# One weight sum of each Strassen set made in the SBUF ring by an accumulating load instead of DRAM steps, the other sum steps at lower rates

## The chip, the core and the metric

The kernel runs on one core of one Trainium2 chip. The metric is the device time of one execution in microseconds (us); lower is better. A core has a matrix engine (TensorE, "PE" in the profile), a vector engine (DVE), an activation engine (ScalarE, "ACT"), GpSimd ("POOL") and SyncE ("SP"). POOL and SP are used here mostly to issue DMAs. Each engine takes its instructions in program order: one that waits holds up all that stand behind it on that engine.

## The reference

One layer of a decoder in float32, 512 positions of width 1024. What matters for this case is that it is a row of large matrix products with weights that lie in DRAM:

```python
proj = x @ w_in[i]                       # q, k, v of three attention branches, and the gates
...                                      # differential, stick-breaking and dilated attention
merged = (g[:, :, 0] * (o_da @ w_branch_da) + g[:, :, 1] * (o_sb @ w_branch_sb)
          + g[:, :, 2] * (o_dl @ w_branch_dil))
x = layer_norm(DEEPNORM_ALPHA * x + merged @ w_out[i], ln1_g[i], ln1_b[i])
hid = jax.nn.relu(x @ w_up[i])           # 1024 -> 4096
c = jnp.square(hid) @ w_down[i]          # 4096 -> 1024
ple = jax.nn.sigmoid(x @ w_ple_gate[i]) * (p[i] @ w_ple[i])
x = layer_norm(DEEPNORM_ALPHA * x + c + ple, ln2_g[i], ln2_b[i])
```

The branch attentions are the kernel's part up to about 690 us, the MLP (`w_up`, `w_down`) the part from there to the end.

## The kernel before

**Products.** Nearly every large product is done as a 2x2 block product with seven multiplications instead of eight (Strassen's scheme in Winograd's form). Products 1, 2 and 4 use a plain block of the weights; products 5, 6, 7 and 3 use sums of two to four weight blocks. One up set (`up_parts(m)`, m = 0 to 7) and one down set (`down_parts`, m = 0 to 6 as seven products) each take four plain blocks and four sums. In an up set the four sums are called operands 0, 1, 2 and 3, and the plain blocks that stand alone "11", "12" and "22". The text writes u0, u1, ... for up sets and d0, d1, ... for down sets. `group_items` does the same for the queries of the three dilated groups (the tile-group sets, `wq`).

**Chunks and the two rings.** A weight block of 128x1024 float32 (512 KB) is a *chunk*. SP loads it into one of six `raw` slots (`fill`, L194 to L216; the DMA is L213). Then ACT casts it to the high part, `wh<-raw` (L262), and DVE takes the low part, `wl<-raw,wh` (L264); this is called splitting the chunk. `wh` and `wl` have five slots each. PE multiplies each block three times (high by high, high by low, low by high). A `raw` slot is loaded anew only when the chunk in it has no more uses; a `wh`/`wl` slot is written again only when PE has read it.

**Sums in DRAM.** The sums are made beforehand in DRAM tiles (`qsum`, `usum`, `dsum` and a few more) by DMAs that POOL issues: `issue` writes a plain copy (L1249) or an accumulating DMA, which adds a block to what is there (L1247). `sum_steps` lists them: an up set has the eight steps

```python
                yield a1, w[2], False
                yield a3, w[0], False
                yield a1, w[3], True
                yield a3, w[2], True
                yield a2, a1, False
                yield a2, w[0], True
                yield a4, a2, False
                yield a4, w[1], True
```

where True means accumulate. A step that uses what an earlier one wrote waits for that DMA to land. Two sets (in the later part of the list) are worked on in turn, a step of each. The finished sum is loaded by SP like any weight block. How far the list runs is set by a credit: each item of the main loop adds its size times a rate, or 0.78 once the gate products are done, and a step is issued for each whole credit. Besides, every step waits for the fourth last `wl` subtraction that the program wrote ahead of it, so that POOL doesn't run ahead of the main stream.

**Sums in the ring.** A second way exists for the value pairs and the gates: `then_add(c, src)` (L171 to L178). After chunk `c` has been split, POOL issues an accumulating DMA of another weight block into the very `raw` slot that `c` lies in (L176), and a later chunk is split from this slot. The slot stays taken until then. In the gates, such a slot is split for the second time four chunks after the first time or later.

**Order.** One Python loop over items writes all instructions. Each engine's order follows from it; nothing is reordered at run time.

Of the kernel before, what the change touches and what calls it, by code (L numbers as in the profile page):

```python
# [10 lines left out]
F32 = mybir.dt.float32  # L11
# [7 lines left out]
P = 128  # L19
# [36 lines left out]
def trunk(tc, a, out):  # L56
    nc = tc.nc
    es = ExitStack()
    with es:
# [108 lines left out]
        def chunk(src, w):  # L168
            return chunk_of(load(src, w))
# [114 lines left out]
        items = []  # L284
# [66 lines left out]
        HC = slice(256, 512)  # L351
        qsum = [[dram.tile([P, 1024], F32, name=f"qsum{m}_{i}") for i in range(4)] for m in range(3)]

        def group_items(gi, pairs):
# [380 lines left out]
        def seven(forms, operand, bank_of, done):  # L735

            cs = {}
            for p in (1, 2, 7, 6, 4, 5, 3):
                for r in range(2):
# [467 lines left out]
        ND = 8  # L1207
        gsum = [[dram.tile([P, 1024], F32, name=f"gsum{m}_{i}") for i in range(2)] for m in range(2)]
        usum = [[dram.tile([P, 1024], F32, name=f"usum{m}_{i}") for i in range(4)] for m in range(ND)]
        dsum = [[dram.tile([P, 1024], F32, name=f"dsum{m}_{i}") for i in range(4)] for m in range(ND - 1)]  # L1210

        def sum_steps():
            def up_steps(sums, w, flat=False):
                w = [w[i] if flat else w[i].rearrange("p k n -> p (k n)") for i in range(4)]
                a1, a2, a3, a4 = sums
# [17 lines left out]
            def down_steps(m):  # L1233
                w = [a["wd"][m, i].rearrange("p k n -> p (k n)") for i in range(4)]
                b1, b2, b3, b4 = dsum[m]
                yield b1, w[0], False
                yield b3, w[1], False
                yield b1, w[1], True
                yield b3, w[3], True
                yield b2, b1, False  # L1240
                yield b2, w[3], True
                yield b4, b2, False
                yield b4, w[2], True

            def issue(o, i, plus):
                if plus:
                    i = nc.gpsimd.dma_start(o, i, accum_op=OP.add, max_dma_last_dim=4096)  # L1247
                else:
# [7 lines left out]
                         for n in range(2) for m in range(2))  # L1256
            todo.extend(up_steps(qsum[m], a["wq"][m]) for m in range(3))
            for n in range(3):
                todo.extend(two_steps(msum[n][m], a["wgm"][n, m]) for m in range(2))
                if n:  # L1260
                    todo.append(up_steps(bsum[2 * (n == 1)], a["wbq"][int(n == 1)]))
# [50 lines left out]
        def up_parts(m):  # L1312
# [5 lines left out]
            def operand(n):  # L1318
                src = usum[m][n] if isinstance(n, int) else wu[{"11": 0, "12": 1, "21": 2, "22": 3}[n]].rearrange(
                    "p k n -> p (k n)")  # L1320
                cs[n] = chunk(src, 1024)

            def pair(j):
# [21 lines left out]
                def part_a():  # L1345
# [632 lines left out]
        def dil_head(hd):  # L1978
# [198 lines left out]
        for n, it in enumerate(items):  # L2177
# [199 lines left out]
```

## Time and profile before

| what | value |
|---|---|
| time, median of three runs | 1036.29 us (1035.86 to 1038.79) |
| time of the profiled execution | 1029.26 us |
| its span in the profile | 1027.5 us |
| granted TensorE clock | 0.999 |
| PE busy | 1014.6 us (99%) |
| DVE busy / ACT busy | 794.4 us (77%) / 614.7 us (60%) |
| POOL busy | 208.8 us (20%) |
| DMA moved | 275.99 MB, 269 GB/s on average |

The busy time of an engine is the time in which one of its instructions ran. The profiled execution lies 7.03 us below the median of the three runs; 1.76 us of it lie outside the span. Of the DMA traffic, 135.08 MB went through the queue that POOL issues to and 138.99 MB through that of SP.

### The profile page before, as it was taken

The page shows a single profiled execution, that of the slowest core. Times are in us where ns is not written, and L with a number is a line of the kernel's source. Part 1 is how long each engine was busy: PE and PEld are TensorE (multiplying, and loading weights), DVE is VectorE, ACT ScalarE, POOL GpSimd, SP SyncE. Part 2 cuts the span into 40 slices and gives each one's busy share as a digit, 9 for nine tenths or more (in the row PEclk, how much of TensorE's full clock was granted, in tenths as well). Part 3 has the DMA queues.
Part 4 walks back from the last instruction along what each step waited for, and adds up shares of the span by engine and source line. Part 5 has one row for each costly group of instructions (what it writes and reads, how often), then busy time and mean ns, then how long its engine had stood idle before and what let it go on. Part 6 is the DMA issues. An engine that isn't in the chain of part 4 may idle for free.

```text
span 1027.5 us, 15644 instructions
## 1 busy us (share of the span) xinstructions
PE 1014.6 (99%) x5626; PEld 879.0 (86%) x5626; DVE 794.4 (77%) x1411; ACT 614.7 (60%) x1055; POOL 208.8 (20%) x311
## 2 busy tenths in 40 slices
PE   9999999999999999999999999999999999999997
PEld 6888887888998898888888888889999999999786
DVE  6888697788657776886788885897778778768785
ACT  7566566775544656566655733866666656556551
POOL 0232320121412123111121130222121211111101
PEclk9999999999999999999999999999999999999999
DMA  8999993888999999879999893799999999998932
GB/s 312 286 306 288 259 271 96 209 206 259 288 319 283 253 287 276 220 201 263 352 291 273 294 323 109 182 248 355 338 323 332 318 324 350 327 332 263 297 148 82
DMA packets 79885, 275.99 MB, mean 269 GB/s; under 512 B 9816, under 2 KB 10600, under 8 KB 79808
## 3 DMA queue, kind: packets, MB, share of 16 engines
q0 software_dynamic: 37712, 135.08, 52.4%
q1 hardware_dynamic: 41520, 138.99, 36.6%
q8 instruction: 44, 0.72, 0.3%
q10 hardware_dynamic: 576, 0.92, 0.2%
q14 instruction: 33, 0.27, 0.1%
HBM read 267.59 MB, written 116.42 MB: 374 GB/s over the span
## 4 chain that ended last, share of the span: by engine, by line
PE 92%; DVE 4%; DMA 1%; ACT 1%; issue 1%; DVEq 0%; SPq 0%; ACTq 0%
PE mm L87 9%; PE mm L88 9%; PE mm L89 9%; PE at L1431 4%; PE at L1430 4%; PE at L1432 4%; PE at L752 2%; PE at L751 2%; PE at L750 2%; PE mm L750 2%; PE mm L751 2%; PE mm L752 2%; PE at L89 2%; PE at L88 2%; PE at L87 2%; PE at L1042 1%
## 5 line engine op out<-in xcount | busy, mean ns | idle before, releaser
L264 DVE TENSOR_TENSOR wl<-raw,wh 128x1024 fp32r<-128x1024 f32 (+1 forms) x274 | 330.2, 1214 | 111.4 <-ACT wh L262 110.2
L262 ACT CAST wh<-raw 128x1024 fp32r<-128x1024 f32 (+1 forms) x274 | 283.7, 1042 | 206.9 <-PE mm L88 104.3
L87 PE MATMUL mm<-xhT,wh 128*128 128x512 f32 (+1 forms) x254 | 95.5, 376 | 1.1 <-DVE dl_k L346 1.1
L89 PE MATMUL mm<-xhT,wl 128*128 128x512 f32 (+1 forms) x254 | 94.4, 371 | 0.0
L88 PE MATMUL mm<-xlT,wh 128*128 128x512 f32 (+1 forms) x254 | 94.1, 370 | 0.0
L1431 PE MATMUL at<-wl,hh 128*128 128x512 f32 x188 | 73.8, 393 | 1.0 <-DVE wl L264 1.0
L1430 PE MATMUL at<-wh,hh 128*128 128x512 f32 x188 | 73.9, 393 | 0.5 <-ACT hid L1402 0.5
L1432 PE MATMUL at<-wh,hl 128*128 128x512 f32 x188 | 73.2, 389 | 0.0
L87 PE MATMUL mm<-x1hT,wh 128*128 128x256 f32 x256 | 72.8, 284 | 0.0
L88 PE MATMUL mm<-x1lT,wh 128*128 128x256 f32 x256 | 72.4, 283 | 0.0
L89 PE MATMUL mm<-x1hT,wl 128*128 128x256 f32 x256 | 72.4, 283 | 0.0
L87 PEld LDWEIGHTS mm<-xhT,wh 128*128 128x128 f32 x254 | 47.9, 189 | 8.9 <-issue 1.2
L89 PEld LDWEIGHTS mm<-xhT,wl 128*128 128x128 f32 x254 | 47.8, 188 | 8.3
L88 PEld LDWEIGHTS mm<-xlT,wh 128*128 128x128 f32 x254 | 47.9, 189 | 7.5
L1247 POOL DMA_DIRECT2D usum<-in_wu_dram x32 | 27.0, 843 | 134.5 <-DVE wl L264 61.5
L87 PEld LDWEIGHTS mm<-x1hT,wh 128*128 128x128 f32 x256 | 48.9, 191 | 1.9
L88 PEld LDWEIGHTS mm<-x1lT,wh 128*128 128x128 f32 x256 | 48.9, 191 | 1.5
L89 PEld LDWEIGHTS mm<-x1hT,wl 128*128 128x128 f32 x256 | 48.9, 191 | 0.0
L1247 POOL DMA_DIRECT2D dsum<-in_wd_dram x28 | 24.1, 860 | 106.4 <-DVE wl L264 30.1
L1432 PEld LDWEIGHTS at<-wh,hl 128*128 128x128 f32 x188 | 35.3, 188 | 7.6
L1430 PEld LDWEIGHTS at<-wh,hh 128*128 128x128 f32 x188 | 35.5, 189 | 7.1 <-ACT hid L1402 0.7
L1431 PEld LDWEIGHTS at<-wl,hh 128*128 128x128 f32 x188 | 35.5, 189 | 7.0 <-DVE wl L264 1.3
(676 smaller groups left out, 2857.3 us busy)
## 6 DMA issues: line engine op xcount, KB each, us to landing
usum<-in_wu_dram POOLq DMA_DIRECT2D x48, 512.0 KB, 8.9
dsum<-in_wd_dram POOLq DMA_DIRECT2D x42, 512.0 KB, 8.9
raw<-usum SPq DMA_DIRECT2D x32, 512.0 KB, 8.5
raw<-dsum SPq DMA_DIRECT2D x28, 512.0 KB, 7.8
raw<-in_wt_dram SPq DMA_DIRECT2D x26, 512.0 KB, 7.8
raw<-in_wd_dram SPq DMA_DIRECT2D x25, 512.0 KB, 9.7
raw<-in_wu_dram SPq DMA_DIRECT2D x24, 512.0 KB, 8.3
qsum<-in_wq_dram POOLq DMA_DIRECT2D x18, 512.0 KB, 8.9
```

Of the source, the lines that this page charges most:

```text
L87: nc.tensor.matmul(ps, wh, xh, start=start, stop=False, skip_group_check=True)
L88: nc.tensor.matmul(ps, wh, xl, start=False, stop=False, skip_group_check=True)
L89: nc.tensor.matmul(ps, wl, xh, start=False, stop=stop, skip_group_check=True)
L262: i = nc.scalar.copy(h, raw)
L264: i = nc.vector.tensor_sub(lo, raw, h.bitcast(F32))
L750: nc.tensor.matmul(ps, h[:, q], c["h"][:, n], start=go, stop=False, skip_group_check=True)
L751: nc.tensor.matmul(ps, h[:, q], c["l"][:, n], start=False, stop=False, skip_group_check=True)
L752: nc.tensor.matmul(ps, lo[:, q], c["h"][:, n], start=False, stop=end, skip_group_check=True)
L1247: i = nc.gpsimd.dma_start(o, i, accum_op=OP.add, max_dma_last_dim=4096)
L1430: nc.tensor.matmul(ps, h[:, q], c["h"][:, s], start=go, stop=False, skip_group_check=True)
L1431: nc.tensor.matmul(ps, h[:, q], c["l"][:, s], start=False, stop=False, skip_group_check=True)
L1432: nc.tensor.matmul(ps, lo[:, q], c["h"][:, s], start=False, stop=end, skip_group_check=True)
```

## The change

In three families of sets one of the four sums is no longer made in DRAM:

- in the three `wq` sets, product 3's sum is made from product 6's chunk by `then_add` (plus `w[1]`);
- in all eight up sets, operand 2 is made from the plain chunk "11" (plus `wu[2]`), and for this "11" is loaded and split ahead of "12" (before: "12", "11", then 2, 1, 0, 3, "22");
- in the down sets d0 to d4, product 4's sum is made from product 6's chunk (plus `wd[m, 2]`). The order of products stays 1, 7, 6, 4, 5, 2, 3. d5 and d6 keep their four sums.

So 32 of 208 POOL steps in DRAM go (6 of 24 for `wq`, 16 of 64 for up, 10 of 56 for down), 16 loads by SP go, and 16 accumulating DMAs into `raw` slots come, issued by POOL. The number of matmuls stays the same. The rates at which the remaining steps are issued are lowered (1.0 to 0.8; 2.8, 2.3 and 3.3 to 2.6, 2.1 and 2.7; 0.78 to 0.6), and the dilated head 3 is put off by one more item.

```diff
@@ group_items
-                    at = {5: 0, 6: 1, 7: 2, 3: 3}.get(p)
-                    cs[p] = [chunk(w[{1: 0, 2: 1, 4: 3}[p]] if at is None else qsum[gi][at], 1024)]
+                    at = {5: 0, 6: 1, 7: 2}.get(p)
+                    cs[p] = [then_add(cs[6][0], w[1]) if p == 3 else
+                             chunk(w[{1: 0, 2: 1, 4: 3}[p]] if at is None else qsum[gi][at], 1024)]
...
-                    items[-1]["rate"] = 1.0
+                    items[-1]["rate"] = 0.8
...
-            it.setdefault("rate", 2.8 if j < 12 else 2.3 if j < 52 else 3.3)
+            it.setdefault("rate", 2.6 if j < 12 else 2.1 if j < 52 else 2.7)
@@ sum_steps
+                a3 = sums[2] if third else None
                 yield a1, w[2], False
-                yield a3, w[0], False
+                if third:
+                    yield a3, w[0], False
                 yield a1, w[3], True
-                yield a3, w[2], True
+                if third:
+                    yield a3, w[2], True
                 yield a2, a1, False
                 yield a2, w[0], True
-                yield a4, a2, False
-                yield a4, w[1], True
+                if fourth:
+                    yield sums[-1], a2, False
+                    yield sums[-1], w[1], True
...
-                yield b4, b2, False
-                yield b4, w[2], True
+                for b4 in dsum[m][3:]:
+                    yield b4, b2, False
+                    yield b4, w[2], True
...
-                todo.append(up_steps(usum[m], a["wu"][m]) if kind == "u" else down_steps(m))
+                todo.append(up_steps(usum[m], a["wu"][m], False, True) if kind == "u" else down_steps(m))
@@ up_parts
+                if n == 2:
+                    cs[n] = then_add(cs["11"], wu[2].rearrange("p k n -> p (k n)"))
+                    return
...
-                    operand(("12", "11")[j])
+                    if j == 0:
+                        operand("11")
+                        operand("12")
@@ down_parts
-                            cs[p] = [down_chunk(m, p) for m in ms]
+                            cs[p] = [down_chunk(m, p) if p != 4 else
+                                     then_add(cs[6][n], a["wd"][m, 2].rearrange("p k n -> p (k n)"))
+                                     for n, m in enumerate(ms)]
@@ the dilated heads, and the main loop
-            for _ in range({0: 6, 1: 2, 3: 1}.get(hd, 0)):
+            for _ in range({0: 6, 1: 2, 3: 2}.get(hd, 0)):
...
-                credit += 0.78
+                credit += 0.6
```

POOL's order around u1 and u2 is the first place to look at. Before, there stand only sum steps for sets that come later:

```order
L1249 DMA dsum2_1_160<-dsum2_0_159 128x1024
L1247 DMA usum4_2_137<-in_wu_dram 128x1024
L1247 DMA dsum2_1_160<-in_wd_dram 128x1024
L1249 DMA usum4_1_136<-usum4_0_135 128x1024
L1249 DMA dsum2_3_162<-dsum2_1_160 128x1024
L1247 DMA usum4_1_136<-in_wu_dram 128x1024
```

After, the additions into the ring stand between them. Of the `raw` tiles, 1497 holds "11" of u0, 1512 that of u1, 1551 that of u2, and 1548 product 6's sum of d0; L1256 is now the copy, L1254 the accumulating step.

```order
L176 DMA raw_1497_7058<-in_wu_dram 128x1024
L1256 DMA dsum2_1_147<-dsum2_0_146 128x1024
L1254 DMA usum4_0_128<-in_wu_dram 128x1024
L1254 DMA dsum2_1_147<-in_wd_dram 128x1024
L1256 DMA usum4_1_129<-usum4_0_128 128x1024
L1254 DMA usum4_1_129<-in_wu_dram 128x1024
L176 DMA raw_1512_7151<-in_wu_dram 128x1024
L1256 DMA usum4_2_130<-usum4_1_129 128x1024
L1256 DMA usum5_0_131<-in_wu_dram 128x1024
L1254 DMA usum4_2_130<-in_wu_dram 128x1024
L1254 DMA usum5_0_131<-in_wu_dram 128x1024
```

The row for `raw_1512` now stands behind a copy that reads `usum4_0` and an addition to the copy, `usum4_1`. The rows that follow, up to u2's addition, are these:

```order
L1256 DMA usum5_1_132<-usum5_0_131 128x1024
L1256 DMA dsum3_0_149<-in_wd_dram 128x1024
L1254 DMA usum5_1_132<-in_wu_dram 128x1024
L176 DMA raw_1548_7434<-in_wd_dram 128x1024
L1256 DMA usum5_2_133<-usum5_1_132 128x1024
L176 DMA raw_1551_7440<-in_wu_dram 128x1024
```

Here too the ring's additions follow a copy of a sum and the step that the copy reads.

The second place is ACT in u1. Before, operand 2 (`raw_1521`) comes by an SP load; its cast is followed by the evacuation of a product's bank (`hid<-mm`):

```order
L262 CAST wh_1548_7407<-raw_1521_7223 128x1024
L1402 ACTIVATE hid_1536_7273<-hid_1536_7273 128x512
L1403 ACTIVATE hid_1536_7273<-hid_1536_7273 128x512
L1398 ACTIVATE hid_1535_7272<-mm_1526_7234 128x256
L291 CAST hh_1557_7488<-hid_1533_7270 128x512
L262 CAST wh_1551_7467<-raw_1524_7229 128x1024
```

After, the cast reads the slot that the addition wrote, `raw_1512`, and the evacuation stands right behind it:

```order
L1415 ACTIVATE hid_1532_7238<-hid_1532_7238 128x512
L262 CAST wh_1542_7368<-raw_1512_7151 128x1024
L1410 ACTIVATE hid_1531_7237<-mm_1522_7199 128x256
L291 CAST hh_1552_7451<-hid_1529_7235 128x512
L262 CAST wh_1546_7430<-raw_1517_7188 128x1024
```

The cast moved behind two activations and is otherwise at the same place in the row; what it waits for changed from an SP load to a POOL addition.

More of the change, by code (lines that the diff above doesn't have):

```diff
@@ L351, in trunk @@
         HC = slice(256, 512)
-        qsum = [[dram.tile([P, 1024], F32, name=f"qsum{m}_{i}") for i in range(4)] for m in range(3)]
+        qsum = [[dram.tile([P, 1024], F32, name=f"qsum{m}_{i}") for i in range(3)] for m in range(3)]
         def group_items(gi, pairs):
@@ L1208, in trunk, with up_steps @@
         gsum = [[dram.tile([P, 1024], F32, name=f"gsum{m}_{i}") for i in range(2)] for m in range(2)]
-        usum = [[dram.tile([P, 1024], F32, name=f"usum{m}_{i}") for i in range(4)] for m in range(ND)]
-        dsum = [[dram.tile([P, 1024], F32, name=f"dsum{m}_{i}") for i in range(4)] for m in range(ND - 1)]
+        usum = [[dram.tile([P, 1024], F32, name=f"usum{m}_{i}") for i in range(3)] for m in range(ND)]
+        dsum = [[dram.tile([P, 1024], F32, name=f"dsum{m}_{i}") for i in range(3 if m < 5 else 4)] for m in range(ND - 1)]
         def sum_steps():
-            def up_steps(sums, w, flat=False):
-                w = [w[i] if flat else w[i].rearrange("p k n -> p (k n)") for i in range(4)]
-                a1, a2, a3, a4 = sums
+            def up_steps(sums, w, third, fourth):
+                w = [w[i].rearrange("p k n -> p (k n)") for i in range(4)]
+                sums = list(sums)
+                a1, a2 = sums[:2]
+                a3 = sums[2] if third else None
                 yield a1, w[2], False
-                yield a3, w[0], False
+                if third:
+                    yield a3, w[0], False
                 yield a1, w[3], True
-                yield a3, w[2], True
+                if third:
+                    yield a3, w[2], True
                 yield a2, a1, False
                 yield a2, w[0], True
-                yield a4, a2, False
-                yield a4, w[1], True
+                if fourth:
+                    yield sums[-1], a2, False
+                    yield sums[-1], w[1], True
             def two_steps(sums, w, flat=False):
@@ L1234, in down_steps @@
                 w = [a["wd"][m, i].rearrange("p k n -> p (k n)") for i in range(4)]
-                b1, b2, b3, b4 = dsum[m]
+                b1, b2, b3 = dsum[m][:3]
                 yield b1, w[0], False
@@ L1256, in sum_steps @@
                          for n in range(2) for m in range(2))
-            todo.extend(up_steps(qsum[m], a["wq"][m]) for m in range(3))
+            todo.extend(up_steps(qsum[m], a["wq"][m], True, False) for m in range(3))
             for n in range(3):
```

4 lines of the change are left out of this document (2 added, 2 removed).

## The prediction, as it was written before the result was known

> **What bounds the kernel now.** I read the page first: how busy each engine is, and the chain of work that ended last.
>
> ```profile
> PE 1014.6 (99%) x5626; PEld 879.0 (86%) x5626; DVE 794.4 (77%) x1411; ACT 614.7 (60%) x1055; POOL 208.8 (20%) x311
> PE 92%; DVE 4%; DMA 1%; ACT 1%; issue 1%; DVEq 0%; SPq 0%; ACTq 0%
> ```
>
> PE is busy for 1014.6 of 1027.5 us. The change leaves all matmuls in place, so it can win only idle time of PE, and it loses whatever idle time it adds. The list of PE's waits says what idle time there is; these two rows are the ones in the MLP, and they lie at its end:
>
> ```profile
> PE at L1431 <- DVE wl L264: 1.0, 1, 1.0
> PE at L1430 <- ACT hid L1402: 0.5, 1, 0.5
> ```
>
> The whole list holds some 6 us, the larger part at the start and in the attention. The third view, busy time by stretch, gives the MLP up to those waits (PE, PEld, DVE, ACT, POOL busy, clock, DMA share, GB/s):
>
> ```profile
> 690.00:970.00 280.00, 280.00 (x1846) 257.68 (x1845) 214.62 (x277) 172.27 (x263) 52.18 (x78) 1.00 1.01 324
> ```
>
> Here PE never idles and the DMA engines are busy all the time: transfers are long, but early enough. So the question is whether the new transfers are still early enough.
>
> **How long a transfer takes, and who waits for whom on POOL.** From the list of DMA issues (median us from issue to landing), the additions into the ring that exist already; then, for all DMAs that touch `usum` in this stretch, the least, median and most; then POOL's waits in it (total, times, longest):
>
> ```profile
> raw<-in_wv_dram POOLq DMA_DIRECT2D x8, 512.0 KB, 7.6
> raw<-in_wgm_dram POOLq DMA_DIRECT2D x12, 512.0 KB, 9.1
> DMA to landing us min/median/max: 4.3/8.7/14.4
> POOL usum L1249 <- DMA usum<-in_wu_dram: 21.8, 5, 7.3
> POOL usum L1247 <- DMA usum<-usum: 20.1, 4, 9.5
> ```
>
> POOL is busy 20% of the time and still not free: its next instruction stands waiting for the landing of the one before it in the same sum. Before, that hurts nobody, since these sums are needed two sets later. After, additions for the present set stand behind such waits. I take 7.6 us from issue to landing for every POOL DMA, the first row, an addition of the new kind; the ends are 4.3 (the shortest seen) and 9.1.
>
> In the gates, where this form stands already, there is room: the addition into the ring is issued at 536.61, lands some 8 us later, and the second cast of that slot runs at 545.57, held by PE (its bracket) and not by the DMA.
>
> ```profile
> 536.61 0.90 POOL L176 DMA_DIRECT2D raw<-in_wgm_dram  x1 [4.21 <-DVE wl L264]
> 545.57 1.06 ACT L262 CAST wh<-raw 128x1024 fp32r<-128x1024 f32 x1 [0.77 <-PE at L752]
> ```
>
> There the second split comes four chunks after the first. In the up sets it now comes two after it.
>
> **The change part by part.** 32 DRAM steps and 16 loads fewer, 16 additions more. All are DMAs beside a full PE, so the saving is worth nothing by itself; its cover is the ring, which the 280.00 of 280.00 us above show as deep enough. The lower rates and the later head 3 move steps that PE doesn't wait for: 0, but for 0.4 us below. "11" ahead of "12": both are loaded before PE needs them, 0. What costs is the wait of ACT's cast for the addition. Behind this cast stand evacuations without which PE can't start a product in the same bank. At each place I ask: when does the addition land, how much ACT work lies from this cast to the evacuation, when does PE need it?
>
> *u0.* Base "11" takes the split that ends second in the DVE row below, 690.46 + 2.35 = 692.8 (the order puts "11" where "12" was). The addition lands at 692.8 + 7.6 = 700.4. Then ACT runs the cast (1.05) and the five rows shown, 4.2 us in all without idle time and with the small overlaps; the copy ends at 704.6. PE needs it at 702.95: **1.7 us** late.
>
> ```profile
> 690.46 2.35 DVE L264 TENSOR_TENSOR wl<-raw,wh 128x1024 fp32r<-128x1024 f32 x2
> 697.56 0.60 ACT L1131 ACTIVATE sg<-at 128x512 f32<-128x512 f32 x1 [0.29 <-PE at L1171]
> 698.96 1.05 ACT L262 CAST wh<-raw 128x1024 fp32r<-128x1024 f32 x1 [0.80 <-PE at L1171]
> 700.32 1.05 ACT L262 CAST wh<-raw 128x1024 fp32r<-128x1024 f32 x1 [0.31 <-PE at L1171]
> 701.27 0.59 ACT L1131 ACTIVATE sg<-at 128x512 f32<-128x512 f32 x1
> 701.76 0.36 ACT L1358 COPY up<-mm 128x256 f32<-128x256 f32 x1
> 702.95 0.28 PE L87 MATMUL mm<-x1hT,wh 128*128 128x256 f32 x1
> ```
>
> *u1.* The evacuation (716.95 before) stands right behind the cast: 1.05 + 0.36 = 1.4 us from landing to end. PE needs it at 720.48, so the addition must land by 719.1. Were POOL free, it would be issued at the end of the base's split, 711.46 + 1.23 = 712.7, and land at 720.3, 1.2 late.
>
> ```profile
> 701.20 2.35 DVE L264 TENSOR_TENSOR wl<-raw,wh 128x1024 fp32r<-128x1024 f32 x2
> 711.46 1.23 DVE L264 TENSOR_TENSOR wl<-raw,wh 128x1024 fp32r<-128x1024 f32 x1 [3.04 <-ACT wh L262]
> 716.95 0.36 ACT L1398 ACTIVATE hid<-mm 128x256 f32<-128x256 f32 x1
> 720.48 0.28 PE L87 MATMUL mm<-x1hT,wh 128*128 128x256 f32 x1
> 717.59 0.81 POOL L1247 DMA_DIRECT2D usum<-in_wu_dram  x1 [1.88 <-DVE wl L264]
> ```
>
> But POOL isn't free. In its new order the addition to `usum4_0` waits for the first split of the row at 701.20, 702.4; the copy to `usum4_1` waits for that to land; the addition to `usum4_1` waits for the copy to land; then comes u1's addition, 0.8 us later (the last row gives the issue time of one). It lands at 702.4 + 0.8 + 3 x 7.6 = 726.0: 6.9 us late.
>
> *u2.* From the cast of operand 2 to the end of the copy that PE needs at 753.26 lie 751.10 + 0.35 - 748.16 = 3.3 us, so the addition must land by 750.0.
>
> ```profile
> 748.16 1.04 ACT L262 CAST wh<-raw 128x1024 fp32r<-128x1024 f32 x1
> 751.10 0.35 ACT L1358 COPY up<-mm 128x256 f32<-128x256 f32 x1
> 753.26 0.28 PE L87 MATMUL mm<-x1hT,wh 128*128 128x256 f32 x1
> ```
>
> In POOL's order seven landings in a row lie between 702.4 and u2's addition (`usum4_0` +, `usum4_1`, `usum4_1` +, `usum4_2`, `usum5_0` +, `usum5_1`, `usum5_1` +), and its own is the eighth; twice one stands behind another issue (0.8 and 0.5). It lands at 702.4 + 1.3 + 8 x 7.6 = 764.5, **14.5 us** late; u1's 6.9 are part of this, since PE has then lost them already. With 5.8 us from issue to landing, nothing would be late here; with 9.1, 26.5 us.
>
> *u3.* The base's split ends at 771.46 + 1.23 = 772.7. After seven landings that chain has fewer steps behind one another, and I take POOL as free: landing 780.3. The cast and what follows take 782.30 + 0.35 - 777.46 = 5.2 us, to 785.5, and PE needs it at 783.08: **2.4 us**.
>
> ```profile
> 771.46 1.23 DVE L264 TENSOR_TENSOR wl<-raw,wh 128x1024 fp32r<-128x1024 f32 x1 [0.54 <-ACT wh L262]
> 777.46 1.05 ACT L262 CAST wh<-raw 128x1024 fp32r<-128x1024 f32 x1 [2.65 <-PE mm L88]
> 782.30 0.35 ACT L1358 COPY up<-mm 128x256 f32<-128x256 f32 x1
> 783.08 0.28 PE L87 MATMUL mm<-x1hT,wh 128*128 128x256 f32 x1
> ```
>
> *u5 and u7.* By the same sum for u5: 849.43 + 1.22 + 7.6 = 858.3, plus 860.63 + 0.36 - 856.76 = 4.2 makes 862.5 against 861.84: **0.6 us**. u7 is laid out alike, another **0.6**.
>
> ```profile
> 849.43 1.22 DVE L264 TENSOR_TENSOR wl<-raw,wh 128x1024 fp32r<-128x1024 f32 x1
> 856.76 1.03 ACT L262 CAST wh<-raw 128x1024 fp32r<-128x1024 f32 x1
> 860.63 0.36 ACT L1358 COPY up<-mm 128x256 f32<-128x256 f32 x1
> 861.84 0.28 PE L87 MATMUL mm<-x1hT,wh 128*128 128x256 f32 x1
> ```
>
> *The rest.* d0's addition is part of u2's chain. For u4 with d1 and d2, for u6 with d3 and d4, and for the `wq` sets, where more chunks lie between, I take 1 us, 0 and 1 us; the ends are 0 and 2.4 each, the largest of the places with a free POOL. What is behind a stalled cast is late next: DVE's `wl`, then PE; and a slot that is held longer delays SP's next load, which is in no term.
>
> *What is won.* At the end, the addition that finishes `dsum6_2` is issued at 940.58; only when it has landed is SP let go, and that load (the chain of waits) brings the two PE waits quoted at the top.
>
> ```profile
> 940.58 0.82 POOL L1247 DMA_DIRECT2D dsum<-in_wd_dram  x1 [0.41 <-issue]
> 947.84 5.94 DMA raw<-dsum
> ```
>
> In the new order this step stands ahead of u6's additions, some five chunks earlier: -1.5 us. A 0.4 us wait in head 3 may go with its delay.
>
> **Sum.** 1.7 + 14.5 + 2.4 + 1.2 + 2 - 1.9 = 19.9, so +20 us. The profiled execution takes 1029.26 us and would take about 1049; the median of the runs shown is 7.0 above the profiled execution, and on that scale 1036.3 + 20 = **1056 us**.
>
> [...]
>
> **Rivals.**
> 1. *Faster: the additions land in time.* The point from which it decides is 5.3 us from issue to landing at u1, (719.1 - 703.2) / 3, and 5.8 at u2. For it: an up set and a down set go from 8 steps and 8 loads to 6, 7 and 1, so the DMA share of 1.01 falls; and the least seen is 4.3. Against it: the median of 8.7. Then only the 1.9 us are left, at 1034 us. Chance 0.16.
> 2. *No change.* PE at 280.00 of 280.00 hides all of it and the end's wait only moves elsewhere: 1036 us. Against it: ACT's order. Chance 0.06.
> 3. *Half.* While PE stands, the ring is full and SP issues nothing, so the transfers on POOL's chain get shorter, say 6.3 us (between 4.3 and 8.7): u2 is 4.1 late, u3 1.1, u0 0.4, the rest 0 to 2, less 1.9: about +5, to +10 if the `wq` sets or u4 lose a little. 1044 us. Chance 0.20.
> 4. *Much slower.* Transfers stay at 8.7 to 9.1: u2 23 to 26 late, the chain reaches u4 as well, and every free place loses 1.1 to 1.5 more: +33 to +38, 1071 us. Chance 0.15.
>
> The forecast keeps 0.43, with 1049 to 1066 as its own range (7.0 to 8.4 us from issue to landing).
>
> **How the numbers follow.** A measurement of this kernel can tell about 0.3%, or 3 us, from no change. Faster is rival 1, except that part of it lies within 3 us: 0.15; same is rival 2 and that part: 0.07; slower is the forecast with rivals 3 and 4: 0.78. The range runs from 1036 (leaving out most of rival 1) to 1072 (leaving out the worst of rival 4).
>
> **What would show it.** Right: PE idles at its first matmul of "12" in u1 and near the second product of u2, waiting for an ACT evacuation; ACT's cast just ahead of it waits for `raw<-in_wu`; POOL's L176 rows come 8 to 20 us after their base's split. The two waits at the end are gone. Wrong: L176 is issued right after the base's split, and casts wait for PE as before; then POOL's DMAs land in under 6 us. A new wait on SP's loads would be a cost that I left out.

## The result, and the profile after

The changed kernel takes **1086.04 us** (median of 4 executions, 1084.11 to 1087.3) against 1036.37 us for the kernel before beside it: a ratio of 1.0473, 95% interval 1.0449 to 1.0496. It is slower, as forecast, but by 49.7 us instead of 20, and above the range. Its profiled execution took 1086.72 us (span 1085.0, granted clock 0.978), 57.5 us of span more than that of before, which lies 7 us under its own median. The traces are compared with each other, so the sums below are made against 57.5.

Busy time and the chain of the changed kernel, the two lines read first:

```profile
PE 1028.4 (95%) x5626; PEld 890.7 (82%) x5626; DVE 796.2 (73%) x1411; ACT 613.6 (57%) x1055; POOL 201.0 (19%) x295
PE 66%; DMA 12%; issue 9%; DVE 6%; ACT 3%; POOL 2%; POOLq 0%; DVEq 0%; ACTq 0%; SPq 0%
```

PE's share of the chain fell from 92% to 66%, and DMA's rose from 1% to 12%. PE is also busy for 13.8 us longer than before (1014.6) with the same 5626 matmuls. The same 280 us of the MLP in which PE never idled (PE, PEld, DVE, ACT, POOL busy, clock, DMA share, GB/s):

```profile
690.00:970.00 280.00, 240.81 (x1515) 220.01 (x1514) 178.46 (x230) 142.46 (x217) 48.21 (x67) 0.93 0.91 261
```

PE's waits (engine, waited for: total, times, longest). Both waits at the end of the MLP, 1.0 and 0.5 us before, are no longer in the list; these are:

```profile
PE mm L87 <- ACT up L1368: 21.3, 6, 9.9
PE mm L87 <- ACT hid L1410: 17.0, 3, 9.9
PE at L2051 <- DVE r L2043: 3.8, 1, 3.8
PE mm L87 <- DVE dl_q L399: 1.2, 1, 1.2
```

The first two rows are the evacuations that the prediction named. What the evacuation waited for stands on ACT and POOL. At u1, in order of time (start, duration, engine, what; in brackets the idle time ahead and what ended it):

```profile
737.20 0.81 POOL L1254 DMA_DIRECT2D usum<-in_wu_dram  x1 [6.51 <-DMA usum<-usum]
737.82 1.08 POOL L176 DMA_DIRECT2D raw<-in_wu_dram  x1
746.33 1.04 ACT L262 CAST wh<-raw 128x1024 fp32r<-128x1024 f32 x1 [12.46 <-DMA raw<-in_wu_dram]
747.28 0.38 ACT L1410 ACTIVATE hid<-mm 128x256 f32<-128x256 f32 x1
747.71 0.58 PE L87 MATMUL mm<-x1hT,wh 128*128 128x256 f32 x1 [9.88 <-ACT hid L1410]
```

POOL stands 6.51 us for a sum's copy to land, then issues the sum's addition and, right behind, the addition into the ring. ACT idles 12.46 us for the latter, the evacuation runs at once after the cast, and PE, which has idled 9.88 us, starts. This is the forecast's picture. At u0 and u5 POOL isn't late to issue; there the transfer itself takes long. First u0, then u5, and then the two transfers as pieces of the chain (start, duration):

```profile
699.97 0.82 POOL L1254 DMA_DIRECT2D dsum<-in_wd_dram  x1 [8.74 <-DVE wl L264]
700.49 0.83 POOL L1256 DMA_DIRECT2D usum<-in_wu_dram  x1
701.02 1.19 POOL L176 DMA_DIRECT2D raw<-in_wu_dram  x1
714.34 1.04 ACT L262 CAST wh<-raw 128x1024 fp32r<-128x1024 f32 x1 [9.57 <-DMA raw<-in_wu_dram]
718.14 0.37 ACT L1368 COPY up<-mm 128x256 f32<-128x256 f32 x1
718.57 0.58 PE L87 MATMUL mm<-x1hT,wh 128*128 128x256 f32 x1 [7.93 <-ACT up L1368]
```

```profile
895.22 0.83 POOL L1254 DMA_DIRECT2D usum<-in_wu_dram  x1 [6.01 <-DVE wl L264]
895.76 1.99 POOL L1254 DMA_DIRECT2D dsum<-in_wd_dram  x2
896.98 1.68 POOL L176 DMA_DIRECT2D raw<-in_wu_dram  x1
913.41 1.04 ACT L262 CAST wh<-raw 128x1024 fp32r<-128x1024 f32 x1 [10.71 <-DMA raw<-in_wu_dram]
917.71 0.58 PE L87 MATMUL mm<-x1hT,wh 128*128 128x256 f32 x1 [9.86 <-ACT up L1368]
```

```profile
701.02 13.21 DMA raw<-in_wu_dram
...
896.98 16.35 DMA raw<-in_wu_dram
```

At u5 four DMAs are issued within 1.8 us. They land 8.3, 11.1, 14.1 and 16.35 us after their own issue, one after the other, with the addition into the ring last.

The longer busy time of PE comes from the clock. PE alone in stretches around the gaps at u0, u1 and u2, and behind a short one in u3 (length, PE busy, granted clock, DMA share, GB/s):

```profile
709.00:718.00 9.00, 1.63 (x14) 0.86 0.56 169
718.00:722.00 4.00, 3.43 (x16) 0.50 0.66 226
722.00:726.00 4.00, 4.00 (x34) 0.96 0.86 174
...
750.00:753.00 3.00, 3.00 (x16) 0.50 0.82 261
753.00:757.00 4.00, 4.00 (x35) 1.00 0.88 312
...
784.00:787.00 3.00, 3.00 (x12) 0.50 1.01 371
787.00:790.00 3.00, 1.96 (x13) 0.98 0.99 176
...
826.00:830.00 4.00, 4.00 (x35) 1.00 0.94 330
```

Behind the gap at u0 PE gets through 16 matmuls in 3.43 us of work; in the next 4 us it gets through 34. The gap ahead of the stretch from 784 us was only 3.0 us long. There are six gaps of 3.0 us or more: 7.93 (u0), 9.88 (u1), 3.01 (u2), 4.08 (u3), 9.86 (u5) and, with the `wq` sets at 273 us, 3.82, together 38.6 us. Spread over them, 13.8 us of longer busy time is 2.3 us per gap. After a gap of 0.93 us, which ends at 825.36 us, it didn't fall, as the last row shows. In this trace the clock stood at 0.50 from 275.1 to 282.0 us (`wq`), 715.5 to 722.3 (u0), 742.8 to 753.0 (u1), 783.7 to 787.1 (u2), 821.3 to 824.7 (u3) and 910.0 to 923.7 (u5); it was full again 3 to 6 us after the end of each gap. How long a gap has to be was not shown. In the kernel without sum steps below, where one wait of PE is 4.3 us and no other above 1.8, the span without the listed waits is 6.8 us longer than before (1045.7 - 17.2 against 1027.5 - 5.8), at a mean clock of 0.992; that is more than 2.3 us for one gap, so by this estimate shorter waits cost clock too. In the kernel before with a credit of 1.1 (last experiment), with one wait of 2.2 us, the same difference is 0.5 us (1028.2 - 6.0), at 0.998.

So the 57.5 us are 38.6 of long gaps, 13.8 of clock behind them, and some 5 of waits of about 1 us and less, the 1.5 us won at the end already taken off.

### The profile page after: what moved, and what is told of

The parts are those of the page before. It is cut to its first block, busy times and chain, and to the rows that moved or that the text cites. A ratio compares the mean times of both kernels' runs of the same rounds, so it can differ in the third digit from the quotient of the medians.

```text
span 1085.0 us, 15598 instructions
## 1 busy us (share of the span) xinstructions
PE 1028.4 (95%) x5626; PEld 890.7 (82%) x5626; DVE 796.2 (73%) x1411; ACT 613.6 (57%) x1055; POOL 201.0 (19%) x295
## 4 chain that ended last, share of the span: by engine, by line
PE 66%; DMA 12%; issue 9%; DVE 6%; ACT 3%; POOL 2%; POOLq 0%; DVEq 0%; ACTq 0%; SPq 0%
PE mm L87 8%; DMA raw<-in_wu_dram 7%; PE mm L88 7%; PE mm L89 7%; PE at L1442 3%; PE at L1443 3%; PE at L1444 3%; DVE wl L264 2%; DMA dsum<-in_wd_dram 2%; PE at L751 2%; PE at L752 2%; PE at L753 2%; ACT wh L262 2%; DMA raw<-in_wq_dram 2%; PE mm L753 1%
## 5 line engine op out<-in xcount | busy, mean ns | idle before, releaser
L87 PE MATMUL mm<-x1hT,wh 128*128 128x256 f32 x256 | 77.4, 302 | 38.3 <-ACT up L1368 21.3
L87 PEld LDWEIGHTS mm<-x1hT,wh 128*128 128x128 f32 x256 | 52.8, 206 | 42.2 <-ACT up L1368 23.1
L88 PE MATMUL mm<-x1lT,wh 128*128 128x256 f32 x256 | 76.2, 298 | 0.0
L89 PE MATMUL mm<-x1hT,wl 128*128 128x256 f32 x256 | 76.2, 298 | 0.0
L88 PEld LDWEIGHTS mm<-x1lT,wh 128*128 128x128 f32 x256 | 52.9, 207 | 1.4
L89 PEld LDWEIGHTS mm<-x1hT,wl 128*128 128x128 f32 x256 | 52.9, 207 | 0.0
L1254 POOL DMA_DIRECT2D usum<-in_wu_dram x24 | 20.2, 855 | 113.4 <-DVE wl L264 77.2
L1930 ACT ACTIVATE lg<-lg,mx 128x128 f32<-128x128 f32 (+3 forms) x32 | 17.7, 555 | 27.5 <-DVE mx L1928 27.5
```

Source lines behind the costliest of these rows:

```text
L87: nc.tensor.matmul(ps, wh, xh, start=start, stop=False, skip_group_check=True)
L88: nc.tensor.matmul(ps, wh, xl, start=False, stop=False, skip_group_check=True)
L89: nc.tensor.matmul(ps, wl, xh, start=False, stop=stop, skip_group_check=True)
```

## The experiments

Each ratio is to the kernel before on the same chip, with its 95% interval; times are medians. Edits are shown against the kernel named. For some kernels a table below splits the delay of the ring's additions in two parts.

**One family at a time.** The kernel before with the old rates, plus one family of the change.

> The kernel before with the change of the up sets alone (operand 2 by an addition into the ring), at the old rates. Theory A (ACT stands at the cast of a chunk whose addition is late, and the evacuations PE needs stand behind it): most of the MLP's loss is here, about 30 us idle and 10 us of lower clock, 1070 to 1080 us. Theory B (the lower rates bring the sum steps too late): no change within 5 us, 1036 us. Theory C (slots of the raw ring are held too long and SP's loads come late): 10 to 20 us, and PE's waits end at an SP load.

> The kernel before with the change of the down sets alone, at the old rates. Theory A: here four or more chunks stand between the two splits of a slot, so little is lost: 0 to 5 us, 1036 to 1041 us. Theory B: no change. Theory C: the slots of the down sets are held longest, so the loss would be largest here, above 10 us.

> The kernel before with the change of the three wq sets alone, at the old rates. Theory A: the two new waits of the changed kernel near 273 and 307 us, 5 us, and 2 us of lower clock: 1040 to 1045 us. Theory B: no change.

```diff
@@ p_up: the kernel before, and only
+                if n == 2:
+                    cs[n] = then_add(cs["11"], wu[2]...)
@@ p_down: the kernel before, and only
-                            cs[p] = [down_chunk(m, p) for m in ms]
+                            cs[p] = [down_chunk(m, p) if p != 4 else then_add(cs[6][n], a["wd"][m, 2]...) ...]
@@ p_q: the kernel before, and only
+                    cs[p] = [then_add(cs[6][0], w[1]) if p == 3 else ...
```

Up alone: 1110.82 us, 1.0709 (1.0687 to 1.0731). Down alone: 1081.53, 1.0428 (1.0405 to 1.0451). `wq` alone: 1043.96, 1.0072 (1.0049 to 1.0096). The MLP's waits of PE in the first, then in the second:

```profile
PE mm L87 <- ACT up L1366: 45.7, 6, 15.7
PE mm L87 <- ACT hid L1408: 22.3, 2, 11.9
```

```profile
PE mm L87 <- ACT hid L1399: 48.0, 3, 20.7
```

Two expectations were missed. The down sets were held to be safe because of four or more chunks between the two splits. In the order of ACT's casts the second split comes only two chunks after the first in d0 and three in d1 to d4, hardly more than the two of most up sets. PE loses 48 us in three waits, since the additions are issued 14 to 21 us after the base's split. And at the old rates up alone is worse than the whole change with its lower ones, and down alone nearly as bad.

**The rate.** The changed kernel with the old rates: is the lower pace a cost?

> The changed kernel with the old rates (0.78, 1.0, 2.8, 2.3, 3.3). Theory A: the sum steps are further ahead in POOL's order and the additions still stand behind some of them; the loss stays within a third of what it is, 1070 to 1095 us. Theory B: the loss goes, 1036 to 1045 us.

```diff
-                credit += 0.6
+                credit += 0.78
```

(and 1.0, 2.8, 2.3, 3.3 back). 1103.27 us, 1.0649 (1.0598 to 1.07). That is above the expected range. The theory that the slower pace costs falls: it saves 17 us.

**POOL without other work in the MLP.** If the additions are late because of POOL's other DMAs, they must be in time when there are none. This kernel issues no DRAM sum step in the MLP; its later sets load the sums of other sets, so the same number of loads, casts and matmuls remains, with wrong sums in part of the sets.

> The changed kernel without any sum step in DRAM once the gate products are done, so that POOL issues nothing in the MLP but the additions into the ring and four constants; the later sets load finished sums of other sets in place of their own, so all loads, casts and matmuls stay. Theory A (the additions are late because of the other DMAs on POOL's queue): they are issued within 1 us of the base's split and land in 5 to 8 us; PE's waits in the MLP shrink from 40 us to under 8, and the time is 1040 to 1052 us, the wq sets' loss among it. Theory C (the distance between the two splits of a slot is too short whatever POOL does): waits of 20 us or more stay, above 1060 us.

```diff
-                src = usum[m][n - (n == 3)] ...
+                src = usum[m % 4][n - (n == 3)] ...
-            src = dsum[m][{5: 0, 6: 1, 7: 2, 4: 3}[p]] ...
+            src = dsum[0][{5: 0, 6: 1, 7: 2, 4: 2}[p]] ...
-                credit += 0.6
+                credit += 0.0
```

1043.56 us, 1.008 (1.0049 to 1.011). PE's waits, and the ring's additions in the list of DMA issues (count, size, median us to landing):

```profile
PE at L2051 <- DVE r L2043: 4.3, 1, 4.3
PE mm L87 <- ACT up L1368: 4.1, 4, 1.7
PE mm L87 <- ACT hid L1410: 1.8, 1, 1.8
```

```profile
raw<-in_wu_dram POOLq DMA_DIRECT2D x8, 512.0 KB, 7.0
raw<-in_wd_dram POOLq DMA_DIRECT2D x5, 512.0 KB, 5.5
```

So 42.5 of the 49.7 us come from POOL's other DMAs in the MLP. The slot held for longer, the order of "11" and "12" and the accumulating form itself stay in this kernel. What remains, 7 us, is about what `wq` alone costs (7.9), but it doesn't lie there alone: in this trace 6.1 us of waits are at the `wq` sets and 7.0 us, in waits of 0.7 to 1.8 us, in the MLP. So even with POOL otherwise empty the new form isn't faster than before.

**Fewer waits between POOL's steps.** Two edits let POOL issue earlier, with as many steps of the same size: copies that read weights in place of the sum that is just being made (these sums then lack parts), and four sets in work at a time in place of two.

> The changed kernel with as many sum steps of the same size, but the copy from a finished sum is a copy of a weight block (the second and last sums of each set lack a part), so that no step waits for the landing of another sum's addition; the addition to a tile still waits for the copy into it. Theory A1 (POOL stands at the landing of the step before): the additions of u1 and u2 are issued 4 to 8 us earlier, their waits (13 us) go for the most part, 1060 to 1075 us. Theory A2 (the transfer itself is slow because other DMAs of POOL are in flight): no change within 6 us, 1080 to 1092 us.

> The changed kernel with four sets of sums in work at a time instead of two in the last part, so that the steps of a set are further apart in POOL's order; same steps, same bytes, same result. Theory A1: POOL stands less, 1060 to 1075 us. Theory A2: 1080 to 1092 us.

```diff
@@ a_unchain
-                yield a2, a1, False
+                yield a2, w[2], False
...
-                    yield sums[-1], a2, False
+                    yield sums[-1], w[3], False
...
-                yield b2, b1, False
+                yield b2, w[0], False
@@ a_run4
-                while todo and len(run) < (4 if len(todo) > 9 else 2):
+                while todo and len(run) < (4 if len(todo) > 9 else 4):
```

1075.76 us, 1.0396 (1.0372 to 1.0419), and 1075.45, 1.0394 (1.0365 to 1.0423): 10 us less each. Standing behind another step's landing is real, but as far as these two edits remove it, it is the smaller part.

**What lies ahead of an addition, what behind.** The kernel without sum steps again, with three idle 512 KB copies that POOL issues to DRAM at each up set's addition and at the first of each down pair or single: once ahead of it, once behind it. The traffic is the same. In a first pair of kernels

> As the run without DRAM sum steps in the MLP, but ahead of each up set's addition (and of the first of each down stage) POOL issues three plain copies of 512 KB from a weight block into DRAM tiles that nobody reads, without any wait. Theory A2 (an addition lands late because the DMAs that POOL issued ahead of it are worked off first): each copy puts the landing off by 2.5 to 3.5 us, so the additions take 13 to 16 us instead of 5.4 to 8.4, and the time is 1075 to 1100 us although nothing waits on POOL. Theory A1 (only POOL's waits count): within 10 us of that run, 1044 to 1054 us.

> The same three copies, issued right behind the addition instead of ahead of it. If POOL's transfers are worked off in the order of issue: the additions land as without the copies (5 to 9 us) and the time is 1043 to 1056 us. If all transfers in flight share the engines evenly: they land in 11 to 16 us as with the copies ahead, above 1070 us.

nothing tied the copies to the place, and POOL issued all 33 between 1.3 and 153.6 us. They took 1070.22 us, 1.0317 (1.0292 to 1.0342), and 1072.81, 1.0354 (1.032 to 1.0389), chiefly through a wait of 15.6 and 15.9 us in the attention, and tell nothing of the MLP. They also show that an engine's order isn't always that in which the loop writes its instructions: what nothing ties can be placed much earlier when the program is built. In a second pair each copy waits for the base's split:

> The run without DRAM sum steps in the MLP (1043.6 us) with three plain copies of 512 KB, which nobody reads, issued by POOL between the end of the base's split and the addition, and now tied to that split (in the first try they were issued some 20 to 100 us too early). Theory A2 (an addition lands late because what POOL issued just ahead of it is worked off first): landing 13 to 17 us after the base's split ends in place of 5.4 to 8.4, 1.5 us of it the issue of the copies; PE waits of 5 to 9 us at u0, u1, u3, u5 and u7, 1075 to 1100 us. Theory A1 (only POOL's waits for earlier landings count): 1044 to 1054 us.

> The same copies right behind each addition. If POOL's transfers are worked off in the order of issue: the additions land within 1 us of what they do without copies, 1043 to 1052 us. If all transfers in flight share the DMA engines evenly: they land in 11 to 16 us here too, above 1070 us.

```diff
@@ then_add, ahead (behind: 0 and 3)
+                with tc.issue_after(idle_copies(3 * near, st["low"])):
+                    i = nc.gpsimd.dma_start(s["raw"], src, accum_op=OP.add, max_dma_last_dim=4096)
+                idle_copies(0 * near, getattr(i, "ins", i))
```

Ahead: 1074.42 us, 1.0368 (1.0318 to 1.0417). Behind: 1043.4 us, 1.0076 (1.0044 to 1.0107), no more than with no copies at all. The ring's additions in the list of DMA issues, with the copies ahead and then with the copies behind:

```profile
raw<-in_wu_dram POOLq DMA_DIRECT2D x8, 512.0 KB, 10.6
raw<-in_wd_dram POOLq DMA_DIRECT2D x5, 512.0 KB, 9.1
```

```profile
raw<-in_wu_dram POOLq DMA_DIRECT2D x8, 512.0 KB, 7.2
raw<-in_wd_dram POOLq DMA_DIRECT2D x5, 512.0 KB, 5.9
```

The same DMAs make the additions land some 3 us later at the median when they are issued ahead. Issued behind, and with no other set's copies ahead, they leave the landing as it is without copies (u0: 10.7 us ahead, 5.7 behind, 5.8 with none). So for the landing it isn't the shared traffic: what POOL has issued earlier is worked off first. At u5 of the changed kernel, too, an SP load issued at 903.0 us, six us after the addition, landed at 911.5, ahead of the addition at 913.3.

The 31 us between the two times are not a clean price of the copies, though. Putting the copies ahead also moved other instructions when the program was built. In the kernel with the copies behind, the order on ACT, DVE and PE in the MLP is that of the kernel without sum steps; with the copies ahead it isn't. There PE asks for operand 2 in u0 ahead of the 24 matmuls of "11", some 3 us sooner, and PE's longest row of waits is one for the cast itself:

```profile
PE at L87 <- ACT wh L278: 15.3, 7, 3.5
```

The expected 5 to 9 us per wait did not come, and how the 31 us divide between the late landings and the moved product stays open.

The table shows, in us, the time from the end of the base's split to the issue of the addition, plus that from the issue to the start of the second cast (ACT's n-th cast in the trace matched with the n-th in the program's order). The second number can hold a little of ACT's own delay.

| kernel | u0 | u1 | u2 | u3 | u5 | u7 |
|---|---|---|---|---|---|---|
| changed | 0.7+13.3 | 7.9+8.5 | 7.6+6.8 | 0.3+11.5 | 0.5+16.4 | 0.3+7.5 |
| up alone, old rates | 9.7+8.0 | 8.9+8.2 | 6.5+11.1 | 11.2+8.4 | 16.9+5.8 | 0.3+7.7 |
| four sets in work | 0.3+13.4 | 0.3+9.7 | 7.2+10.1 | 0.3+11.4 | 0.3+12.1 | 0.3+6.2 |
| no sum steps | 0.3+5.9 | 0.3+5.5 | 0.3+6.4 | 1.1+8.5 | 0.3+6.8 | 0.3+7.7 |
| copies ahead | 1.9+10.8 | 2.6+8.9 | 1.8+12.6 | 1.8+9.9 | 1.8+10.5 | 1.8+10.4 |
| copies behind | 0.3+5.8 | 0.3+5.4 | 0.3+10.0 | 0.3+5.6 | 0.3+7.2 | 0.3+7.4 |

There are two forms of one backlog. At the old rates the additions are issued late, behind steps that wait for landings. At the lower rates, or with four sets in work, most are issued in time and land late, behind transfers issued just before. (u2's 10.0 in the last row stands behind d0's three copies, issued 2.5 to 3.6 us earlier.)

**Order of the operands.**

> The changed kernel with operand 1 loaded and split ahead of operand 2 in each up set, so that three chunks instead of two stand between the split of the base and the waiting cast, and one cast less stands behind it. Theory A: each of the large waits in the up sets shrinks by 1 to 1.5 us and DVE gets one chunk more ahead; 1072 to 1082 us. If the place of the cast doesn't matter: 1083 to 1089 us.

```diff
-                    add((2, 1), mm, ev, bank("y", at_bank))
+                    add((1, 2), mm, ev, bank("y", at_bank))
```

1083.2 us, 1.0468 (1.044 to 1.0496). Its interval covers that of the changed kernel: one chunk later is not enough.

**Keeping POOL quiet ahead of an addition.** No step is written while one of the next five chunks is a base; once with two sets in work, once with four.

> The changed kernel, but in the MLP no sum step is written into POOL's order while one of the next five chunks to be split is a base of an addition (the steps come later, none is dropped). Theory A2 (the addition is slow because other DMAs of POOL are in flight ahead of it): the additions of u0 and u5, which took 13 and 16 us, land in 7 to 9 us, their waits of 8 and 10 us shrink to 2 to 4, and the time is 1060 to 1072 us. Theory A1 (only the landing waits in POOL's order count): 1080 to 1090 us, since the same steps wait for each other.

> The same with four sets of sums in work at a time, so that a step rarely waits for the step before it. Theories A1 and A2 together: 1048 to 1062 us, and PE's waits in the MLP under 15 us. If one of them is the whole cause: no better than the better of the two single runs (1075 us for the four sets alone).

```diff
-            while credit >= 1:
+            while credit >= 1 and not (n > ple_at and any(
+                    c.get("then") for c in chunks[st["split"]:st["split"] + 5])):
```

1102.79 us, 1.0644 (1.0612 to 1.0676), and 1093.49, 1.056 (1.0523 to 1.0596): both missed, worse than without the edit. The held steps come out in a burst, of which these four rows show one:

```profile
803.68 0.82 POOL L1254 DMA_DIRECT2D usum<-in_wu_dram  x1 [6.46 <-DVE wl L264]
804.22 1.96 POOL L1254 DMA_DIRECT2D dsum<-in_wd_dram  x2
805.28 1.44 POOL L1256 DMA_DIRECT2D dsum<-in_wd_dram  x1
```

Four DMAs stand at once; the `usum` step lands after 7.4 us, the three `dsum` steps after 14.1 at the median, and u3's addition, the next one, is issued only 7.3 us after its base's split.

**Up and down without `wq`.** At the lower rate in the MLP, and as before ahead of it.

> The kernel before with the change of the up and down sets, 0.6 a step in the MLP, and nothing changed ahead of the MLP (the wq sets and the rates there as before). If the losses of the parts add up: the changed kernel less the wq sets' 5 to 8 us, 1077 to 1082 us. If not, the wq sets' delay shifts the MLP's pattern and the time can come out on either side by more than 10 us.

```diff
@@ the changed kernel
-                    cs[p] = [then_add(cs[6][0], w[1]) if p == 3 else ...
+                    (as in the kernel before; rates before the MLP too)
```

1070.26 us, 1.0329 (1.0293 to 1.0364). That is 16 us under the changed kernel, where `wq` alone costs 7.9: the parts don't add up. Its PE waits in the MLP are 30.8 us against 38.3, so part of the rest lies in how POOL's list stands when the MLP begins. How much of that the rates ahead of the MLP make, and how much `wq`, stays open.

**The rate alone, in the kernel before.** The two end waits went with an earlier finish of the sums; the kernel before can have that by its rate.

> The kernel before with 0.9 in place of 0.78 as the credit of an item in the MLP: the last sum step comes earlier and the wait of 1.5 us at the end goes. 1033 to 1036 us; no change within the measurement if the wait only moves.

> The kernel before with a credit of 1.1 an item in the MLP (0.9 gave 1030.6 us). The wait at the end is gone already at 0.9, so nothing more is to be won in the trace: 1028 to 1034 us; above 1036 us if the denser steps slow the loads.

```diff
@@ the kernel before
-                credit += 0.78
+                credit += 0.9      # b_11: 1.1
```

With 0.9: **1030.61 us**, 0.9945 (0.9927 to 0.9964), the best of all kernels here, and less than the expected 1033 to 1036. With 1.1: 1031.69, 0.9947 (0.9927 to 0.9968). PE's list with 0.9 begins so, and the two end waits are not in it:

```profile
PE at L1627 <- DVE zero L1624: 1.2, 1, 1.2
PE mm L87 <- DVE dl_k L346: 1.1, 1, 1.1
PE at L1944 <- ACT scr L1949: 0.7, 1, 0.7
```

The spans of the two profiled executions differ by 1.5 us (1026.0 and 1027.5), just these waits; the medians differ by 5.5. The granted clock of the 16 executions of before beside it ran from 0.994 to 0.999, and the five longest of them (1037.81 us and more) stood at 0.994 or 0.995; the 11 executions with 0.9 all had 0.998 or 0.999. Of 1015 us of matmuls 0.3% is 3 us. Why the clock is lower in some executions of the kernel before was not shown.

## Why the prediction was right in kind and wrong in size

**Place and mechanism: right.** The forecast was 20 us of idle time, net; there were 43 (38.6 and 5), at the places named. ACT's cast waits for `raw<-in_wu`, the evacuation stands right behind it, PE idles at its first matmul of "12" in u1, and at that of the first or second product in u0, u2, u3 and u5. Both end waits are gone, as costed (-1.5 us).

**How much delay each place bears: right.** From the prediction's rows, u0's addition may land 698.75 - 692.8 = 5.9 us after the base's split, u1's 719.1 - 712.7 = 6.4, u5's 861.84 - 4.2 - 850.65 = 7.0. Measured were 14.0, 16.4 and 16.9 (the sums in the table). The differences, 8.1, 10.0 and 9.9, are PE's gaps: 7.93, 9.88 and 9.86.

**"I take 7.6 us from issue to landing for every POOL DMA": the step that failed.** One price can't stand for every place. The row it came from is a median over additions with other neighbours. The range beside it was off as well: "all DMAs that touch `usum`" counted 29 SP loads with the 32 DMAs of POOL, and the least, 4.3 us, is that of an SP load. The addition shown for the gates, at 536.61, landed after 5.65 us, not some 8. POOL's DMAs alone, in the same stretch of the kernel before:

```profile
DMA to landing us min/median/max: 6.2/10.2/14.4
```

In the changed kernel:

```profile
raw<-in_wu_dram POOLq DMA_DIRECT2D x8, 512.0 KB, 11.3
usum<-in_wu_dram POOLq DMA_DIRECT2D x32, 512.0 KB, 8.2
```

The up sets' additions took 11.3 at the median: 13.2 at u0, 11.4 at u3 and 16.35 at u5, each with three DMAs of POOL still under way ahead of it, but 8.4 at u1 and 6.8 at u2 with one and two. At u0, forecast 1.7 us late, the 5.6 us more make 7.3 of the 7.9; an issue 0.7 us after the split makes the rest. The two idle-copy kernels show the cause of the late landing: what POOL issued just ahead is worked off first (at u0, 10.7 us with three copies ahead, 5.7 with three behind). Of the 37.5 us by which the 57.5 exceed the forecast, 18 are at u0, u3 and u5, 13.8 are the clock and 4 the `wq` sets.

**"I take POOL as free" for u3, u5 and u7.** POOL was indeed free to issue, 0.3 to 0.5 us after the split, but its transfers weren't done. u5 was costed at 0.6 and cost 9.9; u3 at 2.4 and cost 5.0 (4.08 and 0.93); u7 at 0.6 and cost 0.7, with nothing of POOL's under way ahead of it. Free to issue isn't the same as free.

**The chain of landings at u1 and u2: there, but over-counted.** Up to u2, 14.5 us were forecast, without u0; u1 lost 9.88 and u2 4.05 (3.01 and 1.04), 13.9 in all. That the sum agrees is luck. The chain began at 719.88 us and not at 702.4, since its first step waits for a split that stood behind u0's late cast, and by then PE had been held up by the same delay. From there to u2's addition at 778.62 only four of POOL's waits end at a landing (6.51, 4.95, 3.29 and 4.69 us), against seven landings of 7.6 forecast; the `usum` steps in it landed in 3.7 to 7.0 us, but for two of about 10. The two kernels with fewer waits between steps win 10 us, no more. (For u4 with d1 and d2, 1 us was forecast; three waits of 0.8 us came, 2.4 in all.)

**The clock: missing.** 13.8 us of the difference are matmuls at half rate after six gaps. No rival had this, though each of the slower ones opened gaps of this length. It is in the other kernels too: the span of down alone, with three gaps, is 53.3 us longer than before (1080.8 against 1027.5) and its listed waits of PE 46.2 (52.0 against 5.8), which leaves 7.1 us, 2.4 per gap.

**`wq`: 1 us forecast; 5.0 us of waits, and one of the six drops of the clock.** There ACT's cast waits for the addition and DVE's subtraction for the cast; behind it on DVE stands `r` (L2043), for which PE waits 3.8 us:

```profile
274.05 1.04 ACT L262 CAST wh<-raw 128x1024 fp32r<-128x1024 f32 x1 [5.49 <-DMA raw<-in_wq_dram]
275.12 1.23 DVE L264 TENSOR_TENSOR wl<-raw,wh 128x1024 fp32r<-128x1024 f32 x1 [4.11 <-ACT wh L262]
```

**The rates: costed at 0, and a help.** With the old ones the changed kernel takes 17 us more. The forecast priced steps, not how close together they are.

**The rivals.** The first, additions in time, comes true only where POOL has nothing else: 7.0 and 5.5 us at the median then, and 1043.56 us, not faster even so. The fourth, much slower at 1071, was nearest, but by longer transfers all round; the median of the sums' steps, 8.2, was in fact below the 8.9 of before. The shortest addition into the ring in the changed kernel took 5.3 us, just the point from which that first rival decides at u1, and there it took 8.4.

## What to carry to other kernels

Before a load on which PE depends is moved from one queue to another, read from the trace what that queue will have issued in the 10 us ahead of it, in its new order; the median time of a transfer says little beside its place in the row (11.3 us here, with 6.8 at u2 and 16.35 at u5). Filter such a list by the queue that the transfer will use. If such a transfer must go through a busy queue, put it ahead of the bulk work and not behind it; behind three others it took about twice as long here as alone (10.7 against 5.8 us at u0, and 16.35 at u5 in the changed kernel). Price a gap of PE of 3 us or more at its length plus some 2.3 us of half clock (13.8 us over six gaps here), and add up small waits apart from long ones. When a test kernel adds instructions, compare the order on every engine before comparing the times.

## What the runs showed of the hardware that was not expected

- DMAs that POOL issued one right after the other landed one after the other at u5 of the changed kernel: 8.3, 11.1, 14.1 and 16.35 us for four of 512 KB, some 3 us each beside a running kernel. With three copies of this size ahead, u0's addition landed after 10.7 us, with three behind it after 5.7, with none after 5.8.
- The granted clock was 0.50 until 3 to 6 us after the end of each of the six gaps of PE from 3.0 us on in the changed kernel, and 1.00 after gaps of 0.93 (u3) and 1.04 us (u2). Between these lengths the traces leave it open: with waits up to 1.8 us beside one of 4.3, the kernel without sum steps has a mean clock of 0.992, and the kernel before with a credit of 1.1, with one wait of 2.2 us, 0.998.
- SP's loads were quicker in the changed kernel, where less was moved at once (261 against 324 GB/s in the 280 us of the MLP). Before, they took 8.5 and 8.3 us; after:

```profile
raw<-usum SPq DMA_DIRECT2D x24, 512.0 KB, 6.1
raw<-in_wu_dram SPq DMA_DIRECT2D x24, 512.0 KB, 5.2
```
